# Five gather buffers, a float32 activation in the fronts, and all later column one-hots on ScalarE

## The chip, the core and the metric

The kernel runs on one core of a Trainium2 chip. The metric is the device time of one launch in microseconds (us); the median of three runs is quoted. Beside the timed runs there is one profiled execution, in which the hardware recorded when each instruction ran; all rows in this document come from such executions. The core has five engines that work at the same time, each through its own queue in order: TensorE (PE, matrix products; PEld is its weight load), VectorE (DVE), ScalarE (ACT), GpSimd (POOL), and SyncE (SP), which issues plain transfers. An instruction that waits holds everything behind it in its engine's queue.

## What is computed

One inference step of a two-layer decoder for 512 prompt tokens (four tiles of 128) and 8 sample tokens, all in float32. The first layer mixes tokens by a gated MLP, the second by differential attention. Each is followed by a PEER block: every token picks, for 8 heads, the 16 best of 128 x 128 experts, and adds their outputs. The part that matters here is

```
q = (h @ w_q).reshape(T, 8, 2, 128)
s = einsum('thcd,hcnd->thcn', q, keys)            # two lists of 128 scores per head
sv, si = top_k(s, 16)
cand = sv[:, :, 0, :, None] + sv[:, :, 1, None, :]
top_s, pos = top_k(cand, 16)                       # 16 experts: row key i, column key j
g = softmax(top_s)
act = gelu(einsum('thkd,td->thk', u_tab[eidx], h))
y = einsum('thk,thkd->td', g * act, v_tab[eidx])
```

## The kernel before

Each layer of the kernel (`run_layer`) has fronts and a dense part. A front takes a group of tiles through the token mixing (`gmlp` or `attn`), then through the norm, the query product, the scores and the top-k of the PEER block (`peer_front`). Four fronts are numbered by `stage`: 0 and 1 in the first layer (tile 2; tiles 0, 1, 3 and the samples), 2 and 3 in the second (tile 0; tiles 2, 3, 1 and the samples). A front's products run through `dense`: for each of 8, 16 or 32 columns of weight blocks a 128x1024 block `wt` is loaded and multiplied with the activation, transposed, `hT` (up to 392 tokens wide).

There are two forms of such a product. Where the activation is float32, 8 products go straight from `wt`; the compiler makes two instructions of each. Where it is a pair of float32r halves (`hTh`, `hTl`), `split` makes halves of the weights too (`wh` on ACT, `wl` on DVE), and 24 products of one instruction each are made.

The experts of the tiles are summed in two ways. Two of the four tiles of a layer go through **all** 16,384 experts (`dense_peer`), in four quarters of 32 blocks: `acts(q)` makes gelu(u.h) into `W`, `gates(q)` makes the gate weights by products of one-hots (`gi` for the row keys, `ohj` for the column keys, `ps_g`) and multiplies them into `W`, and the quarter's loop sums `W` times the expert outputs into `y`. While a quarter sums, the next one's `acts` and then `gates` run. The last quarter splits its operands (L562 to L571). The other two tiles are **gathered** (`peer_tile`): 512 times a layer an indirect transfer of 128 rows (0.5 MB) is issued on POOL into a tile `gath`, and one DVE instruction consumes it, L712 for u and L719 for v. The `gath` tiles come from a pool of three buffers, so the third-next transfer waits until DVE has consumed this one.

The order is not written by hand. A scheduler orders each queue, and `pace` ties the n-th gather instruction on DVE to the n-th entry of a list of anchors: `tick(ins, k)` enters an instruction k times. An anchor holds a gather back in the order only; nothing waits for it at run time.

```
gb = ctx.enter_context(tc.tile_pool(name="gb", bufs=3))
...
z = V.scalar_tensor_tensor(u, u, 1.0, h, op0=OP.mult, op1=OP.mult, accum_out=act[:, k:k + 1])
pins[layer].append(z.ins)
...
tick(z, [6, 6, 6, 5][stage[0]])
```

Of the kernel before, what the change touches and what calls it, by code (L numbers as in the profile page):

```python
# [8 lines left out]
F32 = mybir.dt.float32  # L9
# [9 lines left out]
D = 1024  # L19
# [16 lines left out]
def body(ctx: ExitStack, tc: tile.TileContext, a):  # L36
# [4 lines left out]
    gb = ctx.enter_context(tc.tile_pool(name="gb", bufs=3))  # L41
# [35 lines left out]
    HB, NW = [4], [264]  # L77
# [105 lines left out]
    def split_T(name, both=False):  # L183

        if stage[0] == 2 or 1 and not stage[0]:
            return wa.tile([128, 8, 128], F32, name=name, tag="h", bufs=HB[0])
        pool, tag, n = (per, "hT", 392) if stage[0] else (wa, "hA", 256)
        if [0, 0, 0, 0][stage[0]] and not both:
            return pool.tile([128, 8, n], F32, name=name, tag=tag + "h", bufs=1)
        return [pool.tile([128, 8, n], FR, name=name + k, tag=tag + k, bufs=1) for k in "hl"]  # L190
# [20 lines left out]
    def dense(w, nk, rhs, n, consume, f0=0, f1=None, steps=None):  # L211

        f1 = w.shape[0] if f1 is None else f1
        for f in range(f0, f1):
            ps = pm.tile([128, 512], F32, name="ps_d", tag="mm")
            for c0 in range(0, nk, 8):
# [9 lines left out]
                else:  # L226
# [3 lines left out]
                    tick(z, [6, 6, 6, 5][stage[0]])  # L230
# [3 lines left out]
    def to_tok(n, tiles, func, tok):  # L234
        hold = {}

        def consume(ft, ps):
            q, i = divmod(ft, ZF)
            if i == 0:
                hold[0] = wa.tile([128, ZF, NW[0]], F32, name="zT", tag="zT", bufs=3)  # L240
# [23 lines left out]
    def gmlp(tiles, n, ph):  # L264
# [54 lines left out]
        def u_out(ft, ps):  # L319
            if ft % ZF == 0:  # L320
                hold[0] = wa.tile([128, ZF, NW[0]], F32, name="uT", tag="zT", bufs=3)
# [36 lines left out]
    def topk_rank(s, p, nh, state, h0):  # L358
# [14 lines left out]
        cand = wk.tile([128, nh, 88], F32, name="cand", tag=f"cand{nh}", bufs=1)[:p]  # L373
# [92 lines left out]
    def dense_peer(layer, dpa, open_rest, open_odd, smp):  # L466
        hT = dd["hT"]
        NQ, QI, NV = 4, 32, 4
# [4 lines left out]
        def acts(q):  # L473

            W[q] = (odd if q % 2 else dpa).tile([128, QI, 256], F32, name="W", tag="W", bufs=1)
            for il in range(QI):
# [3 lines left out]
                if (il * 5) % 32 < [[0, 16, 32, 32], [0, 16, 32, 32]][layer][q]:  # L480
                    uh, ul = split(u, [2, 3][layer] if q else [0, 1][layer])
                    for c in range(8):
                        PE.matmul(ps, uh[:, c, :], hT[0][:, c, :256], start=c == 0, stop=False)  # L483
                        PE.matmul(ps, uh[:, c, :], hT[1][:, c, :256], start=False, stop=False)  # L484
                    for c in range(8):
                        PE.matmul(ps, ul[:, c, :], hT[0][:, c, :256], start=False, stop=c == 7)  # L486
                else:
                    for c in range(8):
                        for k in range(2):
                            z = PE.matmul(ps[:, k * 128:(k + 1) * 128], u[:, c, :], hF[k][:, c, :], start=c == k == 0,  # L490
                                          stop=c == 7, skip_group_check=True)
                    tick(z, [2, 3][layer] if q else [0, 1][layer])
# [3 lines left out]
        def gates(q):  # L496
# [4 lines left out]
            for t0 in range(0, 256, 32):  # L501
# [32 lines left out]

        hF = [dpa.tile([128, 8, 128], F32, name=f"hF{k}", tag=['vb', 'vb'][k], bufs=3 if ['vb', 'vb'][k] == "vb" else 1)
              for k in range(2)]
        for k in range(2):
            V.tensor_tensor(hF[k], *[z.bitcast(F32)[:, :, k * 128:(k + 1) * 128] for z in hT], op=OP.add)  # L538
# [50 lines left out]
    def peer_front(tiles, n, layer, ph):  # L589
        if any(t == 4 or t not in DT[layer] for t in tiles):  # L590
            gbc = bcast_row(a["f_norm_g"][layer], D, f"g_f{layer}")
        hT = dd["hT"] = split_T("hT", True)
# [23 lines left out]
        if 4 in tiles:  # L616
            qz = [wa.tile([128, 8, 72], F32, name=f"qz{c}", tag="zT", bufs=3) for c in range(2)]
# [82 lines left out]
    def gather(table, ix, k, pool=None, tag="sg", nb=1):  # L700
        t = gb.tile([128, D], F32, name="gath", tag="g") if pool is None else \
            pool.tile([128, D], F32, name="gaths", tag=tag, bufs=nb)
# [64 lines left out]
    def run_layer(layer, setup):  # L767
# [11 lines left out]
        HB[0], NW[0] = 4 - layer, GROUPS[layer][1][1]  # L779
# [58 lines left out]
    def setup1(ph):  # L838
# [182 lines left out]
        def attn(tiles, n):  # L1021
# [6 lines left out]
            if first:  # L1028
                hT = per.tile([128, 8, 392], F32, name="hT", tag="hTh")
# [3 lines left out]
                row4 = per.tile([128, 2, D], F32, name="row4", tag="hTl")[:NB]  # L1033
# [16 lines left out]
            def row(t, k):  # L1050
# [153 lines left out]
```

## Time and profile before

| | us |
|---|---|
| three runs | 3499.5, 3507.37, 3507.73; median 3507.37 |
| the profiled execution, its own time | 3478.04 |
| its span, first to last instruction | 3476.3 |
| busy in the span: PE, DVE, ACT, POOL | 3063.4, 2545.1, 1421.2, 1289.9 |

The profiled execution was 0.8% faster than the median of the runs. Busy times of different engines overlap. A busy PE is not a PE at its pace: the ends of matrix products are modelled, and consecutive ones overlap in the records, as DVE's do by some 0.08 us. In the rows, "x<-ps_b" means that x was written from ps_b, and "<-DVE hF L538" behind a time in brackets or a bar names what ended the wait.

### The profile page before, as it was taken

The page shows a single profiled execution, that of the slowest core. Times are in us where ns is not written, and L with a number is a line of the kernel's source. Part 1 is how long each engine was busy: PE and PEld are TensorE (multiplying, and loading weights), DVE is VectorE, ACT ScalarE, POOL GpSimd, SP SyncE. Part 2 cuts the span into 40 slices and gives each one's busy share as a digit, 9 for nine tenths or more (in the row PEclk, how much of TensorE's full clock was granted, in tenths as well). Part 3 has the DMA queues.
Part 4 walks back from the last instruction along what each step waited for, and adds up shares of the span by engine and source line. Part 5 has one row for each costly group of instructions (what it writes and reads, how often), then busy time and mean ns, then how long its engine had stood idle before and what let it go on. Part 6 is the DMA issues. An engine that isn't in the chain of part 4 may idle for free.

```text
span 3476.3 us, 53629 instructions
## 1 busy us (share of the span) xinstructions
PE 3063.4 (88%) x19776; PEld 2450.6 (70%) x19776; DVE 2545.1 (73%) x5191; ACT 1421.2 (41%) x3180; POOL 1289.9 (37%) x1061
## 2 busy tenths in 40 slices
PE   7988948779999999999888888646899999999998
PEld 7887538779757857757878643546899658758656
DVE  1478569888666777668657677779888666777778
ACT  2343022125565485664444344322236334343433
POOL 0034442334344344434320433442334444334343
PEclk9998979889999999999999988769899999999999
DMA  7677875778888989889985777775788889889888
GB/s 257 226 253 253 276 241 189 254 277 284 299 310 308 332 304 320 318 292 327 332 287 179 281 256 248 261 235 176 270 301 311 313 300 321 318 291 341 304 278 316
DMA packets 271576, 976.76 MB, mean 281 GB/s; under 512 B 30938, under 2 KB 31770, under 8 KB 271306
## 3 DMA queue, kind: packets, MB, share of 16 engines
q0 software_dynamic: 152064, 553.72, 46.5%
q1 hardware_dynamic: 119250, 419.62, 34.5%
q8 instruction: 155, 2.54, 0.3%
q14 instruction: 107, 0.88, 0.1%
HBM read 966.76 MB, written 6.46 MB: 280 GB/s over the span
## 4 chain that ended last, share of the span: by engine, by line
PE 37%; DMA 27%; DVE 15%; issue 14%; POOL 6%; ACT 1%; POOLq 0%; DVEq 0%; SPq 0%; ACTq 0%
DMA gath<-peer_v,ix 15%; PE y L573 10%; DMA gath<-peer_u,ix 9%; POOL gath L703 6%; PE ps_d L228 4%; DVE gath L712 3%; PE ps_g L528 3%; DVE x L719 3%; PE ps_a L486 3%; PE ps_a L490 3%; PE ps_a L483 3%; PE ps_a L484 3%; PE y L570 1%; DVE wl L208 1%; PE y L571 1%
## 5 line engine op out<-in xcount | busy, mean ns | idle before, releaser
L703 POOL DMA_INDIRECT gath<-peer_u,ix x512 | 634.2, 1239 | 1212.4 <-DVE gath L712 631.1
L703 POOL DMA_INDIRECT gath<-peer_v,ix x512 | 612.6, 1197 | 910.4 <-DVE x L719 531.4
L712 DVE SCALAR_TENSOR_TENSOR gath<-gath,h_g 128x1024 f32<-128x1024 f32 x512 | 622.9, 1222 | 298.0 <-DMA gath<-peer_u,ix 295.9
L719 DVE SCALAR_TENSOR_TENSOR x<-gath,act,x 128x1024 f32<-128x1024 f32 x512 | 656.2, 1282 | 246.1 <-DMA gath<-peer_v,ix 241.5
L573 PE MATMUL y<-vb,W 128*128 128x512 f32 x1536 | 718.6, 611 | 5.2 <-DVE W L531 5.2
L521 ACT ACTIVATE ohj<-iota,selJ 128x128 f16<-128x128 f32 x1408 | 423.8, 388 | 352.0 <-PE ps_g L528 351.7
L573 PEld LDWEIGHTS y<-vb,W 128*128 128x128 f32 x1536 | 285.4, 196 | 292.6 <-issue 287.2
L490 PE MATMUL ps_a<-hF,ub 128*128 128x128 f32 x3072 | 362.5, 281 | 50.9 <-DVE hF L538 50.3
L490 PEld LDWEIGHTS ps_a<-hF,ub 128*128 128x128 f32 x3072 | 358.6, 198 | 52.7 <-DVE hF L538 50.7
L528 PEld LDWEIGHTS <-ohj 128*128 128x128 f16 x4096 | 257.6, 130 | 94.1 <-issue 86.5
L483 PE MATMUL ps_a<-hTh,wh 128*128 128x256 f32 x1280 | 320.3, 288 | 0.0
L484 PE MATMUL ps_a<-hTl,wh 128*128 128x256 f32 x1280 | 312.4, 282 | 0.0
L528 PE MATMUL ps_g<-gi,ohj 128*128 128x32 f16 x4096 | 269.9, 233 | 11.6 <-DVE gaths L731 8.1
L206 ACT ACTIVATE wh<-ub 128x1024 fp32r<-128x1024 f32 x160 | 169.6, 1060 | 255.0 <-PE ps_a L484 205.0
L483 PEld LDWEIGHTS ps_a<-hTh,wh 128*128 128x128 f32 x1280 | 243.1, 190 | 3.4 <-issue 2.9
L484 PEld LDWEIGHTS ps_a<-hTl,wh 128*128 128x128 f32 x1280 | 242.7, 190 | 3.4 <-issue 3.4
L222 PE MATMUL ps_d<-hTh,wh 128*128 128x392 f32 (+1 forms) x640 | 230.7, 362 | 12.2 <-ACT qT L637 5.3
L223 PE MATMUL ps_d<-hTl,wh 128*128 128x392 f32 (+1 forms) x640 | 226.4, 355 | 3.5 <-DVE hTl L200 3.2
L208 DVE TENSOR_TENSOR wl<-ub,wh 128x1024 fp32r<-128x1024 f32 x160 | 194.9, 1222 | 43.2 <-ACT wh L206 37.8
L531 DVE TENSOR_TENSOR W<-ps_g,W 128x512 f32<-128x512 f32 x128 | 156.7, 1225 | 83.0 <-PE ps_g L528 82.5
L493 ACT ACTIVATE W<-ps_a 128x256 f32<-128x256 f32 x256 | 94.7, 374 | 275.1 <-PE ps_a L490 217.8
L206 ACT ACTIVATE wh<-wt 128x1024 fp32r<-128x1024 f32 x88 | 93.3, 1061 | 242.5 <-PE ps_d L223 168.3
(313 smaller groups left out, 4662.0 us busy)
## 6 DMA issues: line engine op xcount, KB each, us to landing
ub<-peer_ut SPq DMA_DIRECT2D x256, 512.0 KB, 5.2
vb<-peer_v SPq DMA_DIRECT2D x256, 512.0 KB, 5.3
wt<-w_in SPq DMA_DIRECT2D x64, 512.0 KB, 4.5
wt<-peer_wq SPq DMA_DIRECT2D x64, 512.0 KB, 4.3
wt<-w_out SPq DMA_DIRECT2D x32, 512.0 KB, 4.5
gath<-peer_u,ix POOLq DMA_INDIRECT x512, 6.1
gath<-peer_v,ix POOLq DMA_INDIRECT x512, 6.2
wt<-w_k SPq DMA_DIRECT2D x16, 512.0 KB, 5.6
```

What stands on the lines that cost most here:

```text
L206: SC.activation(wh, w, AF.Copy)
L208: tick(V.tensor_tensor(wl, w, wh.bitcast(F32), op=OP.subtract), k)
L222: PE.matmul(ps[:, :n], wh[:, c, :], rhs[0][:, c, :n], start=c == 0, stop=False)
L483: PE.matmul(ps, uh[:, c, :], hT[0][:, c, :256], start=c == 0, stop=False)
L484: PE.matmul(ps, uh[:, c, :], hT[1][:, c, :256], start=False, stop=False)
L490: z = PE.matmul(ps[:, k * 128:(k + 1) * 128], u[:, c, :], hF[k][:, c, :], start=c == k == 0, stop=c == 7, skip_group_check=True)
L521: SC.activation(oh[:, :, k], iota128, AF.Abs, scale=-1.0, bias=selJ[:, t2 + k:t2 + k + 1])
L528: PE.matmul(ps[:, t - t1, :], oh[:, :, k], gi[:, c, :, t - t0], start=c == 0, stop=c == 1)
L573: PE.matmul(y[t][hf], w[:, ts], v[:, hs], start=i == 0, stop=i == 127)
L703: GP.indirect_dma_start(out=t, out_offset=None, in_=table, in_offset=bass.IndirectOffsetOnAxis(ap=ix[:, k:k + 1], axis=0))
L712: z = V.scalar_tensor_tensor(u, u, 1.0, h, op0=OP.mult, op1=OP.mult, accum_out=act[:, k:k + 1])
L719: z = V.scalar_tensor_tensor(x[t], v, act[:, k:k + 1], x[t], op0=OP.mult, op1=OP.add)
```

## The change

The pool of gather buffers has five instead of three. The activation of the query product, and in the second layer of the products by w_k, w_v and w_o as well, is one float32 tile (`full_T`, in the pool `wk`) instead of a pair of halves; only the input product of stage 1 keeps the halves. Of 88 splits of front weights 32 stay. The first quarter's `acts` use that tile in one product of 256 tokens (`hT`) instead of two of 128 (`hF0`, `hF1`, which DVE had to add up first); the later quarters use halves `hP`, made while the second block of the first quarter runs, and all their blocks are split, where half of the second quarter's were not: 192 splits of `ub` instead of 160. From the second quarter on every column one-hot is made on ACT (L521, L524: eight narrow instructions and one wide), where in the second layer half were one DVE instruction each (L515): 80 become 32. The anchors of stage 1's query product grow from 2 to 6 per column of blocks, those of stage 3 become 3. The rest moves memory: three `h` tiles instead of four in the first layer, two `zT` tiles instead of three there, and `row4` goes into the `h` ring.

```
-    gb = ctx.enter_context(tc.tile_pool(name="gb", bufs=3))
+    gb = ctx.enter_context(tc.tile_pool(name="gb", bufs=5))
...
-    HB, NW = [4], [264]
+    HB, NW, ZB = [3], [264], [3]
...
+    def full_T(name):
+
+        if stage[0] % 2 == 0:
+            return wa.tile([128, 8, 128], F32, name=name, tag="h", bufs=HB[0])
+        return wk.tile([128, 8, 392], F32, name=name, tag="hT", bufs=1)
+
+    def split_T(name):
+
+        if stage[0] != 1:
+            return full_T(name)
+        return [pool.tile([128, 8, 392], FR, name=name + k, tag="hT", bufs=1) for k, pool in (("h", wk), ("l", wa))]
...
-                    tick(z, [6, 6, 6, 5][stage[0]])
+                    tick(z, [6, 6, 6, 3][stage[0]])
...
+        hP = [dpa.tile([128, 8, 256], FR, name=f"hP{k}") for k in "hl"]
...
-                if (il * 5) % 32 < [[0, 16, 32, 32], [0, 16, 32, 32]][layer][q]:
-                    uh, ul = split(u, [2, 3][layer] if q else [0, 1][layer])
+                if q:
+                    uh, ul = split(u, [2, 3][layer])
...
-                        for k in range(2):
-                            z = PE.matmul(ps[:, k * 128:(k + 1) * 128], u[:, c, :], hF[k][:, c, :], start=c == k == 0,
-                                          stop=c == 7, skip_group_check=True)
+                        z = PE.matmul(ps, u[:, c, :], hT[:, c, :256], start=c == 0, stop=c == 7)
...
+                    if il == 1:
+                        SC.activation(hP[0], hT[:, :, :256], AF.Copy)
+                        V.tensor_tensor(hP[1], hT[:, :, :256], hP[0].bitcast(F32), op=OP.subtract)
...
-                        if (t2 // 8) % 4 < ([2, 2][layer] if not q else 2 * J_DVE[layer][q]):
+                        if not q and (t2 // 8) % 4 < 2:
...
-        hT = dd["hT"] = split_T("hT", True)
+        hT = dd["hT"] = full_T("hT")
...
-        HB[0], NW[0] = 4 - layer, GROUPS[layer][1][1]
+        HB[0], NW[0], ZB[0] = 3, GROUPS[layer][1][1], 2 + layer
...
-                hT = split_T("hT")
+                hT = full_T("hT")
...
-            oT = split_T("oT")
+            oT = full_T("oT")
```

What the scheduler makes of it, first on DVE at the norm before stage 3's query product: `rs_...` and `r` are the steps of the norm's root, `gath,act<-gath,h_g` is a gather's u instruction. Before:

```order
L128 TENSOR_SCALAR rs_msm<-ss 128x4
L129 TENSOR_SCALAR rs_ym<-rs_msm 128x4
L712 SCALAR_TENSOR_TENSOR gath,act<-gath,h_g 128x1024
L134 TENSOR_TENSOR rs_tm<-rs_ym 128x4
L135 TENSOR_TENSOR rs_tm<-rs_tm,rs_msm 128x4
L712 SCALAR_TENSOR_TENSOR gath,act<-gath,h_g 128x1024
L137 SCALAR_TENSOR_TENSOR rs_ym<-rs_tm,rs_ym 128x4
L134 TENSOR_TENSOR rs_tm<-rs_ym 128x4
L135 TENSOR_TENSOR rs_tm<-rs_tm,rs_msm 128x4
L712 SCALAR_TENSOR_TENSOR gath,act<-gath,h_g 128x1024
L138 SCALAR_TENSOR_TENSOR rs_um<-rs_tm 128x4
L140 SCALAR_TENSOR_TENSOR r<-rs_um,rs_ym 128x4
```

The same place after the change:

```order
L128 TENSOR_SCALAR rs_msm<-ss 128x4
L129 TENSOR_SCALAR rs_ym<-rs_msm 128x4
L134 TENSOR_TENSOR rs_tm<-rs_ym 128x4
L135 TENSOR_TENSOR rs_tm<-rs_tm,rs_msm 128x4
L137 SCALAR_TENSOR_TENSOR rs_ym<-rs_tm,rs_ym 128x4
L134 TENSOR_TENSOR rs_tm<-rs_ym 128x4
L135 TENSOR_TENSOR rs_tm<-rs_tm,rs_msm 128x4
L138 SCALAR_TENSOR_TENSOR rs_um<-rs_tm 128x4
L140 SCALAR_TENSOR_TENSOR r<-rs_um,rs_ym 128x4
L607 SCALAR_TENSOR_TENSOR h_g<-x_78,r,g_f_18047 128x1024
```

The gathers have left the root's steps; here they stand ahead of the last additions to x and behind the norm. Second, DVE at the end of the program, in the last quarter, before (`wl` and `wdl` are the low halves that PE multiplies, `x_78<-gath,act,x_78` a gather's v instruction):

```order
L564 TENSOR_TENSOR wdl<-W,wdh 128x256
L208 TENSOR_TENSOR wl<-vb,wh 128x1024
L719 SCALAR_TENSOR_TENSOR x_78<-gath,act,x_78 128x1024
L564 TENSOR_TENSOR wdl<-W,wdh 128x256
L208 TENSOR_TENSOR wl<-vb,wh 128x1024
L719 SCALAR_TENSOR_TENSOR x_78<-gath,act,x_78 128x1024
```

And after:

```order
L565 TENSOR_TENSOR wdl<-W,wdh 128x256
L211 TENSOR_TENSOR wl<-vb,wh 128x1024
L565 TENSOR_TENSOR wdl<-W,wdh 128x256
L211 TENSOR_TENSOR wl<-vb,wh 128x1024
L565 TENSOR_TENSOR wdl<-W,wdh 128x256
L211 TENSOR_TENSOR wl<-vb,wh 128x1024
```

No gather is left in either layer's last quarter. Counted over DVE's whole queue, the gather instructions (L712 and L719) are spread so; the times are those at which the profiled execution of before passed the marks:

| DVE's queue from ... to ... | us of before | gathers before | after |
|---|---|---|---|
| first gather to the norm before stage 1's query product | 196 to 482 | 103 | 108 |
| to the first multiply of the gates into W (L531) | 482 to 784 | 81 | 121 |
| to the 16th of 64 such multiplies | 784 to 912 | 42 | 45 |
| to the 64th | 912 to 1567 | 211 | 238 |
| last quarter of the first layer, and stage 2 | 1567 to 1830 | 75 | 0 |
| stage 3, to the 9th head's softmax | 1830 to 2033 | 46 | 60 |
| to its 32nd, the last | 2033 to 2173 | 50 | 75 |
| to the norm before stage 3's query product | 2173 to 2285 | 41 | 29 |
| to the second layer's first multiply into W | 2285 to 2584 | 87 | 80 |
| to its 64th | 2584 to 3368 | 253 | 268 |
| last quarter of the second layer | 3368 to 3476 | 35 | 0 |

Between the last multiply of one quarter's gates and the first of the next, where `acts` stands, 38, 37, 38 and 36 gathers become 46, 45, 46 and 47.

## Rows read from the trace of the kernel before

**Rows 1.** The page's first part: busy us, share of the span, instructions.
```profile
PE 3063.4 (88%) x19776; PEld 2450.6 (70%) x19776; DVE 2545.1 (73%) x5191; ACT 1421.2 (41%) x3180; POOL 1289.9 (37%) x1061
```
**Rows 2.** The waits: engine, line, releaser; us in total, times, longest us.
```profile
POOL gath L703 <- DVE gath L712: 732.2, 331, 19.5
...
DVE gath L712 <- DMA gath<-peer_u,ix: 295.9, 212, 4.6
...
DVE x L719 <- DMA gath<-peer_v,ix: 241.5, 198, 6.0
```
**Rows 3.** The DMA issues: count, median us from issue to landing.
```profile
gath<-peer_u,ix POOLq DMA_INDIRECT x512, 6.1
```
**Rows 4.** Busy us (instructions) per stretch: PE, PEld, DVE, ACT, POOL; PEclk, DMA share, GB/s.
```profile
160.00:482.00 322.00, 260.44 (x1272) 217.95 (x1272) 225.69 (x422) 87.05 (x147) 130.69 (x106) 0.90 0.78 261
482.00:784.00 302.00, 230.18 (x1644) 223.89 (x1645) 263.36 (x945) 74.53 (x142) 102.00 (x82) 0.86 0.69 235
784.00:912.00 128.00, 128.00 (x1331) 126.56 (x1330) 107.24 (x128) 81.76 (x205) 53.76 (x42) 1.00 0.82 284
912.00:1662.00 750.00, 727.19 (x4380) 506.58 (x4380) 532.04 (x667) 444.74 (x1038) 316.18 (x257) 0.98 0.89 315
1662.00:1830.00 168.00, 142.21 (x1091) 132.95 (x1090) 94.45 (x218) 77.37 (x210) 47.31 (x41) 0.92 0.83 298
1830.00:2033.00 203.00, 175.93 (x956) 148.24 (x954) 146.66 (x405) 80.49 (x176) 56.25 (x49) 0.94 0.70 236
2033.00:2173.00 140.00, 117.68 (x353) 50.92 (x354) 107.78 (x289) 55.31 (x146) 54.48 (x51) 0.79 0.79 257
2173.00:2285.00 112.00, 55.70 (x277) 50.33 (x275) 84.01 (x131) 31.32 (x46) 52.34 (x41) 0.68 0.77 254
2285.00:2584.00 299.00, 227.44 (x1624) 217.97 (x1625) 270.23 (x950) 73.93 (x140) 105.49 (x89) 0.88 0.72 243
2584.00:3368.00 784.00, 769.12 (x5357) 568.81 (x5355) 581.69 (x723) 322.77 (x745) 332.68 (x268) 0.98 0.88 310
3368.00:3476.30 108.30, 94.92 (x384) 74.61 (x384) 91.57 (x118) 41.98 (x63) 37.40 (x32) 0.94 0.86 305
```
**Rows 5.** Timeline of DVE, 2272 to 2286 us: start, us, what [idle before <-releaser].
```profile
2272.63 1.23 DVE L712 SCALAR_TENSOR_TENSOR gath<-gath,h_g 128x1024 f32<-128x1024 f32 x1 [3.92 <-DMA gath<-peer_u,ix]
...
2276.99 0.17 DVE L128 TENSOR_SCALAR rs_msm<-ss 128x4 f32<-128x4 f32 x1
...
2284.74 0.16 DVE L140 SCALAR_TENSOR_TENSOR r<-rs_um,rs_ym 128x4 f32<-128x4 f32 x1
```
**Rows 6.** PE's waits: us in total, times, longest us.
```profile
PE ps_t L172 <- ACT xr L168: 58.0, 3, 24.9
PE ps_a L490 <- DVE hF L538: 50.3, 2, 25.6
...
PE ps_t L196 <- DVE hTl L179: 26.4, 3, 13.3
```
**Rows 7.** Timeline of PE at 378 and 2255 us: float32 and halves, 392 tokens.
```profile
378.03 6.42 PE L228 MATMUL ps_d<-uv,wt 128*128 128x392 f32 x19
...
2255.71 1.59 PE L225 MATMUL ps_d<-oTh,wl 128*128 128x392 f32 x8
```
**Rows 8.** Groups by line: count | busy us, mean ns of one | idle before.
```profile
L712 DVE SCALAR_TENSOR_TENSOR gath<-gath,h_g 128x1024 f32<-128x1024 f32 x512 | 622.9, 1222 | 298.0 <-DMA gath<-peer_u,ix 295.9
L521 ACT ACTIVATE ohj<-iota,selJ 128x128 f16<-128x128 f32 x1408 | 423.8, 388 | 352.0 <-PE ps_g L528 351.7
...
L524 ACT ACTIVATE ohj<-ohj 128x1024 f16<-128x1024 f16 x176 | 179.6, 1044 | 0.5
...
L208 DVE TENSOR_TENSOR wl<-wt,wh 128x1024 fp32r<-128x1024 f32 x88 | 107.5, 1221 | 11.6 <-ACT wh L206 5.6 <-ACT kq_tok L1044 3.5 <-ACT uv L276 2.2
...
L515 DVE TENSOR_TENSOR ohj<-selb,iotaJ 128x1024 f16<-128x1024 f16 x80 | 54.8, 687 | 19.6 <-PE ps_g L528 19.4
```
**Rows 9.** Busiest stretch of the transfers, same columns as Rows 4.
```profile
1425.00:1440.00 15.00, 15.00 (x109) 12.04 (x108) 12.09 (x15) 4.94 (x9) 6.65 (x6) 1.00 0.99 376
```

More of the change, by code (lines that the diff above doesn't have):

```diff
@@ L239, in consume @@
             if i == 0:
-                hold[0] = wa.tile([128, ZF, NW[0]], F32, name="zT", tag="zT", bufs=3)
+                hold[0] = wa.tile([128, ZF, NW[0]], F32, name="zT", tag="zT", bufs=ZB[0])
             z = hold[0]
@@ L320, in u_out @@
             if ft % ZF == 0:
-                hold[0] = wa.tile([128, ZF, NW[0]], F32, name="uT", tag="zT", bufs=3)
+                hold[0] = wa.tile([128, ZF, NW[0]], F32, name="uT", tag="zT", bufs=ZB[0])
             u = hold[0]
@@ L372, in topk_rank @@
                 yield
-        cand = wk.tile([128, nh, 88], F32, name="cand", tag=f"cand{nh}", bufs=1)[:p]
+        cand = wk.tile([128, nh, 88], F32, name="cand", tag="cand", bufs=1)[:p]
         def add(o, a0, na, nb):
@@ L532, in gates @@
                     yield
[L535 to L538, printed above, removed]
         for _ in acts(0):
@@ L616, in peer_front @@
         if 4 in tiles:
-            qz = [wa.tile([128, 8, 72], F32, name=f"qz{c}", tag="zT", bufs=3) for c in range(2)]
+            qz = [wa.tile([128, 8, 72], F32, name=f"qz{c}", tag="zT", bufs=ZB[0]) for c in range(2)]
             for z in qz:
@@ L698, in sample_finish, with gather @@
         yield
-    def gather(table, ix, k, pool=None, tag="sg", nb=1):
+    def gather(table, ix, k, pool=None):
         t = gb.tile([128, D], F32, name="gath", tag="g") if pool is None else \
-            pool.tile([128, D], F32, name="gaths", tag=tag, bufs=nb)
+            pool.tile([128, D], F32, name="gaths", tag="sg", bufs=1)
         GP.indirect_dma_start(out=t, out_offset=None, in_=table,
@@ L1028, in attn @@
             if first:
-                hT = per.tile([128, 8, 392], F32, name="hT", tag="hTh")
+                hT = wk.tile([128, 8, 392], F32, name="hT", tag="hT", bufs=1)
                 zb = hT[:, :, nq:nq + 256]
@@ L1032, in attn @@
                 hT = hT[:, :, :nq]
-                row4 = per.tile([128, 2, D], F32, name="row4", tag="hTl")[:NB]
                 smp["v"] = ks.tile([128, D], F32, name="v_smp", tag="hs", bufs=1)[:NB]
@@ L1048, in heads, with row @@
                 return [(dst[t][:rows[t]].rearrange("p (h d) -> p h d", d=64), rows[t]) for t in kqv]
-            def row(t, k):
-                return wa.tile([128, D], F32, name="kq_tok", tag="h", bufs=HB[0]) if t < 4 else row4[:, k]
-            kt = {t: row(t, 0) for t in kqv}
+            def row(t):
+                return wa.tile([128, D], F32, name="kq_tok", tag="h", bufs=HB[0])[:rows[t]]
+            kt = {t: row(t) for t in kqv}
             dense_tok(a["w_k"], 8, hT, nq, kqv, AF.Copy, rows_out(kt))
@@ L1062, in attn @@
                     to_T(kt[t], NB, smp["kT"], 0)
-            qt = {t: row(t, 1) for t in kqv}
+            qt = {t: row(t) for t in kqv}
             dense_tok(a["w_q"], 8, hB, nq, kqv, AF.Copy, rows_out(qt))
```

14 lines of the change are left out of this document (4 added, 10 removed).

## The prediction

> **What bounds the kernel now.** I read the busy times first. PE is busy for 88% of the span, DVE for 73%, ACT for 41% [rows 1]; that names no bound yet, since the stages differ. So I cut the span into stretches [rows 4]. In the two dense stretches, 912 to 1662 and 2584 to 3368 us, PE is busy for 727 of 750 and 769 of 784 us: PE sets them. In the fronts it isn't: from 482 to 784 PE has 230 of 302 us, from 2285 to 2584 227 of 299, while DVE has 263 and 270. In these two DVE sets the time (top-k, splits, gathers), and PE waits for what DVE does last. The other stretches are chains: between 2173 and 2285 neither PE (56 of 112) nor DVE (84) is full.
>
> Next the waits. POOL waits 732 us for DVE to give back a gather buffer, at the u gathers alone, and DVE waits 296 + 242 = 538 us for gathered rows [rows 2]. A gather lands 6.1 us after its issue [rows 3] and its DVE instruction takes 1.22 us [rows 8]; with three buffers a round of at least 7.3 us brings three gathers, 2.4 us each, beside a mean of 3.2 (1,024 over the 3,270 us from the first on). The order was made for that pace, and DVE, in order, stands still at each late one with all that is behind it. Where it hurts is seen at the norm ahead of stage 3's query product [rows 5]: nine small steps of 0.16 us, yet between 2272.63 and 2284.90 DVE gets through them only among six gathers, the first after an idle 3.92 us. PE waits for that norm's result: 58 us at three such places, 50 us twice for the sum `hF`, 26 us for the low halves `hTl` [rows 6].
>
> **The change, stretch by stretch.** I sum against the profiled execution, 3478 us; the runs' median is 0.8% above it, and I carry the same difference over to it.
>
> Prices first. A column of blocks with float32 costs PE 6.42 us for 19 instructions, the last one's own 0.5 us included, so 0.329 each and 16 of them 5.26 us; by halves the last eight take 1.59 us, 0.179 each, and 24 of them 4.29 us [rows 7]. So each of the 56 changed columns costs PE 0.97 us **more**, 54 us in all: 16 in stage 1, 40 in stage 3. In return DVE loses 1.22 us per split [rows 8], ACT about as much. A one-hot costs ACT 8 x 0.30 (424 us busy over 1,408) + 1.04 = 3.4 us instead of DVE 0.69 [rows 8]: 48 of them put 165 us on ACT and take 33 off DVE. ACT has 323 of 784 us there; the first layer's later quarters already make all of theirs on ACT, with ACT at 445 of 750 and PE at 97% [rows 4]. I cost this edit at zero, hidden beside PE; if ACT were too late, its bound is the 165 us less what fits, and the first layer speaks for nothing.
>
> *160 to 482.* Five gathers more, but no late ones: two norms have their root among gathers here, and each loses some 8 us of the 12 that rows 5 show. **-16** (bounds -5 and -25; PE's idle time here is 62).
>
> *482 to 784.* DVE sets it. Removed: 16 splits, 19.5 us, and 20 low halves, an estimated 8 us (each writes an eighth to a half of what a split writes in 1.22 us). Added: 40 gathers (81 become 121, since the anchors of stage 1 grow from 2 to 6), at 1.22 us: 49. DVE goes from 263 to 285. Its idle 39 us are mostly late gathers; I leave 23. 308: **+6** (-15, +25). PE's first `acts` start some 25 us earlier without `hF`, for nothing: the gates need DVE's top-k. The 15.5 us more of products are hidden in the same wait.
>
> *784 to 912.* DVE 107 of 128. 13 splits more (all blocks of the second quarter), 16 us, and three gathers, 4: 127. Idle 21 becomes 9: **+8** (-5, +15). PE's savings there give nothing, because DVE is then last.
>
> *912 to 1662.* PE sets it. 38 gathers leave the last quarter, where DVE, with splits and gathers, is what PE waits for; the second layer's shows the price: PE 95 of 108 us, so 12 to 13 us for 35. **-13**. Against it, 16 gathers more stand in the two `acts` pieces, where transfers are densest: 8.4 MB (0.524 each), or 22 us at the 376 GB/s of the busiest stretch [rows 9]; I charge 4 of the 22, since the stretch as a whole has 11% of the transfers' time free [rows 4]. **-9** (-20, +20).
>
> *1662 to 1830.* All 37 gathers go, 45 of DVE's 94 us, and some 20 MB of transfers with them. PE is idle for 26 us; part of that is its own chain. **-11** (0, -20).
>
> *1830 to 2285.* To 2033: 16 columns of stage 3, +15.5 on PE, against half of PE's idle 27: +2. To 2173: 25 gathers more, +31 on DVE's 108, so it nearly fills the 140, and with 13 idle makes 152: +12. To 2285: eight columns, +8; DVE falls from 84 to 54 (8 splits, 8 low halves, 12 gathers less), the norm's root is free of gathers, the transposes need no low half; I take half of PE's idle 56 back: -20. **-6** (-30, +25).
>
> *2285 to 2584.* Like 482 to 784, but the anchors give seven gathers less instead of 40 more. DVE: 16 splits, 20 low halves, 7 gathers, 36 us less: 234, and with half its idle time 249. PE: 227 + 15.5, and 14 for the norm and the transposes: 257. PE is later. **-42** (-20, -55). The 25 us of `hF` and most of the waits for `r` and `hTl` go here.
>
> *2584 to 3368.* 13 splits more and four gathers fewer up to the 16th multiply, 11 us on a DVE that has idle time there: +2; 19 gathers more in the two `acts` pieces, 10 MB or 26 us, of which 6: **+8** (-5, +30). *Last quarter*: **-12** (-5, -15).
>
> Sum: -16 + 6 + 8 - 9 - 11 - 6 - 42 + 8 - 12 = **-74**. 3478 becomes 3404, the median 3507 becomes **3433**. The bounds are independent, so their spread adds in squares: about 50 either way.
>
> **The rivals.**
>
> *DVE gets freer than I think.* Five buffers take away nearly all 538 us of waits. Then 482 to 784 ends 15 us earlier instead of 6 later, 784 to 912 5 earlier, 160 to 482 saves 25, 1830 to 2285 15 more, the last quarters 6 more: 21 + 13 + 9 + 15 + 6 = 64 beyond the forecast, 3369. For it: a round of 7.3 us over five buffers is 1.5 us a gather. Against it: the new order spends the pace at once, 121 gathers in 302 us.
>
> *A deeper queue only lengthens.* If gathers land later in proportion to their number in flight (10 us instead of 6.1), five buffers are as late as three. Then the 16 at 160 to 482 are lost, the idle time that I took off at 482 to 912 (16 and 12) and at 2285 to 2584 (14), and 10 at 2173: 68 of the 74, so 3472, 3501 for the median, and the change does not do what it says. Against it: in the fronts the transfers' engines are busy for 69 to 78% at 235 to 261 GB/s [rows 4], far from 376.
>
> *The transfers are the bound in `acts`.* If those pieces have no room left, the 35 gathers more (18.4 MB) cost their full 49 us at 376 GB/s instead of my 10: -35, 3472 for the median. For it: 0.99 of the engines' time in the busiest stretch [rows 9]. The Trainium skill, DMA: Bandwidth & Descriptors, section Bandwidth, speaks for it too: for transfers from HBM the HBM side binds, at about 358 GB/s for a core; the row's 376 GB/s lies a little above, so the ceiling it names is about where the trace has one, and 18.4 MB would be an estimated 51 us by it.
>
> *PE holds the fronts* (the other side). If PE and not DVE is what ends the fronts, the float32 columns outside 482 to 784 cost their 40 x 0.97 = 39 us openly, and the 75 us that I book in the fronts (16, 11, 6, 42) do not come: 3478 + 1 + 39 = 3518, the median 3547. It decides from the point where PE's idle time in 1830 to 2584, now 177 us, falls by less than 39. For it: float32 is dearer on PE by 23%. Against it: those 177 us [rows 4].
>
> **How the numbers follow.** Forecast (own range 3385 to 3480) 0.50; freer DVE 0.17; transfers in `acts` 0.12; longer queue 0.10; PE 0.11. A difference under 0.3%, some 10 us, can't be told from none here. Faster by more: 0.50 + 0.17 + 0.12 and a third of the longer queue, 0.82; same 0.08; slower 0.10. For 8 in 10 the range goes from 3370, the freer DVE, to 3510, past the longer queue.
>
> **What would show it.** DVE's waits for `gath` fall from 538 to under 200 us, with a landing time under 8 us. The wait for `hF` is gone, and 2285 to 2584's counterpart takes about 257 us, with PE's idle time there halved; 482 to 784's is unchanged within 15. Stage 2 and the last quarters hold no gather, and PE is at 95% or more in the latter. ACT is under 75% in the second layer's gates. Wrong would be: landings of 9 us or more, PE idle in `acts` with waits for `ub` or `wl`, or query products that run without a gap and end later than before.

## The result, and the profile after

The changed kernel takes 3346.91 us (median; 3341.34 to 3354.19, four runs) against 3507.55 us (3499.5 to 3510.39, four runs): ratio 0.9547, 95% interval 0.9523 to 0.9571. It is 161 us faster, where 74 were forecast, and lies 23 us under the range. Its profiled execution took 3354.19 us, 124 less than the one that the forecast was summed on. The direction was right and the size was not.

The page's first part:

```profile
PE 3083.2 (92%) x18048; PEld 2315.2 (69%) x18048; DVE 2464.0 (73%) x5045; ACT 1537.9 (46%) x3586; POOL 1374.2 (41%) x1061
```

Against [rows 1] PE rose from 88% to 92% of a shorter span. The waits of the changed kernel (us in total, times, longest us):

```profile
POOL gath L704 <- DVE x L720: 510.1, 219, 17.9
POOL gath L704 <- DVE ix L672: 490.2, 2, 304.4
POOL gath L704 <- DVE gath L713: 382.8, 185, 14.3
...
DVE gath L713 <- DMA gath<-peer_u,ix: 99.1, 84, 7.5
DVE x L720 <- DMA gath<-peer_v,ix: 49.7, 47, 3.3
...
ACT W L499 <- DVE si L369: 41.7, 2, 23.2
...
PE ps_a L494 <- ACT W L499: 29.3, 2, 16.6
```

DVE's waits for gathered rows are 99 + 50 = 149 us where they were 538 [rows 2]. The stretches, from mark to mark as in [rows 4]:

```profile
161.00:438.00 277.00, 254.49 (x1286) 215.38 (x1284) 228.77 (x434) 85.53 (x145) 157.01 (x111) 0.96 0.86 309
438.00:751.80 313.80, 243.78 (x1050) 185.78 (x1051) 288.88 (x972) 62.65 (x134) 159.84 (x125) 0.86 0.84 300
751.80:881.00 129.20, 119.81 (x1147) 115.21 (x1145) 124.15 (x152) 90.27 (x207) 73.79 (x46) 0.96 0.86 301
881.00:1638.00 757.00, 740.80 (x4456) 522.24 (x4455) 534.52 (x665) 452.77 (x1085) 312.45 (x248) 0.97 0.84 307
1638.00:1768.00 130.00, 122.06 (x1024) 115.81 (x1024) 38.61 (x143) 61.49 (x169) 0.00 (x0) 0.99 0.63 205
1768.00:1963.00 195.00, 183.07 (x823) 123.93 (x821) 139.96 (x380) 61.75 (x155) 82.62 (x65) 0.96 0.82 290
1963.00:2128.00 165.00, 132.94 (x375) 58.68 (x374) 138.00 (x337) 60.89 (x157) 93.99 (x74) 0.73 0.86 299
2128.00:2201.00 73.00, 54.13 (x198) 34.13 (x198) 53.51 (x87) 17.43 (x30) 37.58 (x30) 0.85 0.82 295
2201.00:2478.70 277.70, 240.77 (x1006) 180.31 (x1007) 240.40 (x914) 60.93 (x129) 98.02 (x81) 0.91 0.73 258
2478.70:3255.00 776.30, 764.36 (x5207) 557.71 (x5205) 584.98 (x706) 492.87 (x1190) 357.62 (x278) 0.97 0.87 318
3255.00:3352.50 97.50, 92.02 (x384) 73.52 (x384) 52.78 (x67) 41.96 (x62) 0.00 (x0) 0.97 0.46 151
```

The largest single surprise is the first: 322 us became 277. PE was busy for 260 of the 322 us [rows 4] and is for 254 of the 277; its products in there are the same but for the ends of the window. DVE, by line, in that stretch, in the kernel before and then in the changed one:

```profile
L712 DVE SCALAR_TENSOR_TENSOR gath<-gath,h_g 128x1024 f32<-128x1024 f32 x55 | 67.2, 1225 | 52.0 <-DMA gath<-peer_u,ix 51.7
L719 DVE SCALAR_TENSOR_TENSOR x<-gath,act,x 128x1024 f32<-128x1024 f32 x48 | 61.6, 1283 | 39.1 <-DMA gath<-peer_v,ix 38.4
L208 DVE TENSOR_TENSOR wl<-wt,wh 128x1024 fp32r<-128x1024 f32 x34 | 41.5, 1221 | 3.8 <-ACT uv L276 2.2 <-ACT wh L206 1.4 <-issue 0.2
```

```profile
L713 DVE SCALAR_TENSOR_TENSOR gath<-gath,h_g 128x1024 f32<-128x1024 f32 x60 | 72.3, 1220 | 21.1 <-DMA gath<-peer_u,ix 20.7
L720 DVE SCALAR_TENSOR_TENSOR x<-gath,act,x 128x1024 f32<-128x1024 f32 x48 | 61.5, 1281 | 12.1 <-DMA gath<-peer_v,ix 11.2
L211 DVE TENSOR_TENSOR wl<-wt,wh 128x1024 fp32r<-128x1024 f32 x32 | 39.1, 1221 | 8.0 <-ACT uv L279 4.1 <-ACT wh L209 2.7 <-issue 0.7
```

The work is nearly the same (five gathers more and two splits fewer fall into the window). What differs is the last column: 90 us of waits for rows became 32, and of those 58 us 45 are off the stretch.

Below are the same marks on DVE's timeline (those of the table in the section on the change, named by the times of before) for five kernels; the runs are told in the next section. Lengths in us.

| stretch of before | forecast | before | before, again | changed | changed, again | three buffers | late order, five | no gather transfers |
|---|---|---|---|---|---|---|---|---|
| 0 to 482 | -16 | 482 | 491 | 438 | 437 | 493 | 438 | 441 |
| 482 to 784 | +6 | 302 | 305 | 314 | 314 | 312 | 277 | 294 |
| 784 to 912 | +8 | 128 | 128 | 129 | 129 | 124 | 123 | 118 |
| 912 to 1567 | -20, with the next | 655 | 661 | 653 | 654 | 641 | 633 | 633 |
| 1567 to 1830 | | 263 | 262 | 234 | 233 | 256 | 250 | 233 |
| 1830 to 2285 | -6 | 455 | 465 | 433 | 435 | 495 | 445 | 404 |
| 2285 to 2584 | -42 | 299 | 309 | 278 | 277 | 301 | 275 | 270 |
| 2584 to 3368 | +8 | 784 | 785 | 776 | 776 | 770 | 748 | 751 |
| last quarter | -12 | 109 | 107 | 98 | 98 | 104 | 97 | 97 |
| span | -74 | 3476 | 3512 | 3352 | 3350 | 3497 | 3285 | 3241 |

### The profile page after: what moved, and what is told of

It is laid out like the page before. It is cut to its first block, busy times and chain, and to the rows that moved or that the text cites. A ratio compares the mean times of both kernels' runs of the same rounds, so it can differ in the third digit from the quotient of the medians.

```text
span 3352.5 us, 50442 instructions
## 1 busy us (share of the span) xinstructions
PE 3083.2 (92%) x18048; PEld 2315.2 (69%) x18048; DVE 2464.0 (73%) x5045; ACT 1537.9 (46%) x3586; POOL 1374.2 (41%) x1061
## 4 chain that ended last, share of the span: by engine, by line
PE 64%; DVE 12%; DMA 9%; issue 7%; POOL 4%; ACT 4%; SPq 0%; DVEq 0%; POOLq 0%; ACTq 0%
PE y L574 19%; PE ps_d L231 7%; PE ps_g L534 6%; PE ps_a L488 5%; PE ps_a L489 5%; PE ps_a L491 5%; DMA gath<-peer_u,ix 4%; POOL gath L704 4%; PE ps_a L494 3%; DMA gath<-peer_v,ix 3%; DVE gath L713 2%; DVE x L720 2%; PE y L570 2%; PE y L571 2%; PE y L572 2%
## 5 line engine op out<-in xcount | busy, mean ns | idle before, releaser
L527 ACT ACTIVATE ohj<-iota,selJ 128x128 f16<-128x128 f32 x1792 | 543.8, 388 | 150.4 <-PE ps_g L534 140.9
L231 PE MATMUL ps_d<-hT,wt 128*128 128x128 f32 (+3 forms) x2048 | 430.3, 369 | 25.1 <-DMA wt<-peer_wq 6.8
L488 PE MATMUL ps_a<-hPh,wh 128*128 128x256 f32 x1536 | 402.0, 298 | 11.1 <-ACT wh L209 11.1
L231 PEld LDWEIGHTS ps_d<-hT,wt 128*128 128x128 f32 x2048 | 304.4, 199 | 136.7 <-issue 16.9
L489 PE MATMUL ps_a<-hPl,wh 128*128 128x256 f32 x1536 | 384.7, 287 | 0.0
L488 PEld LDWEIGHTS ps_a<-hPh,wh 128*128 128x128 f32 x1536 | 300.5, 196 | 23.2 <-ACT wh L209 12.7
L489 PEld LDWEIGHTS ps_a<-hPl,wh 128*128 128x128 f32 x1536 | 300.5, 196 | 8.4 <-issue 8.4
L494 PE MATMUL ps_a<-hT,ub 128*128 128x256 f32 x1024 | 234.9, 392 | 29.7 <-ACT W L499 29.3
L494 PEld LDWEIGHTS ps_a<-hT,ub 128*128 128x128 f32 x1024 | 200.4, 197 | 60.8 <-ACT W L499 30.1
L530 ACT ACTIVATE ohj<-ohj 128x1024 f16<-128x1024 f16 x224 | 231.0, 1043 | 0.2
```

The lines of the kernel that those rows point to most:

```text
L231: z = PE.matmul(ps[:, :n], wt[:, c, :], rhs[:, c0 + c, :n], start=c0 + c == 0, stop=c0 + c == nk - 1)
L488: PE.matmul(ps, uh[:, c, :], hP[0][:, c, :], start=c == 0, stop=False)
L489: PE.matmul(ps, uh[:, c, :], hP[1][:, c, :], start=False, stop=False)
L494: z = PE.matmul(ps, u[:, c, :], hT[:, c, :256], start=c == 0, stop=c == 7)
L527: SC.activation(oh[:, :, k], iota128, AF.Abs, scale=-1.0, bias=selJ[:, t2 + k:t2 + k + 1])
L530: SC.activation(oh2, oh2, AF.Relu, bias=1.0, scale=-1.0)
```

## The experiments

**Which part makes the gain.** Two theories stood against each other, A: the buffers; B: the float32 activation, the moved gathers and the one-hots. First the changed kernel with three buffers:

```
-    gb = ctx.enter_context(tc.tile_pool(name="gb", bufs=5))
+    gb = ctx.enter_context(tc.tile_pool(name="gb", bufs=3))
```

> The changed kernel with three gather buffers instead of five and nothing else edited. Theory A (the buffers made most of the gain, because the vector engine's queue stood at late gathers and all of the fronts' work stood behind them): its waits for gathered rows return from 149 us to 400 or more, the stretch from the first gathers to the norm ahead of stage 1's query product, where the change left the products as they were, returns from 277 towards 320 us, and the median lies between 3420 and 3480 us. Theory B (the float32 activation, the moved gathers and the one-hots made it, and five buffers only help): the stretch stays under 290 us and the median lies between 3350 and 3390 us.

3501.27 us (ten runs), ratio to before 0.9997 (0.9976 to 1.0018): without the buffers the whole change is worth nothing. It is above A's own range. DVE's waits:

```profile
DVE gath L713 <- DMA gath<-peer_u,ix: 305.1, 217, 7.1
...
DVE x L720 <- DMA gath<-peer_v,ix: 278.7, 197, 5.1
```

584 us, more than before had. B falls, and the same edit with `bufs=4` shows how fast the gain comes:

> The changed kernel with four gather buffers. At 7.3 us for a round, four buffers allow a gather each 1.8 us, five each 1.5 us, three each 2.4 us, beside a mean of 3.2 us between gathers and 2.6 us in stage 1's query product. Theory A: most of the gain is there with four, as 1.8 lies under both: 3350 to 3385 us, waits for gathered rows 180 to 280 us. If bursts in the order count more than the mean pace, the median lies half way between three and five buffers, 3390 us or more. Theory B: within 10 us of five buffers.

3375.34 us, ratio 0.964 (0.9613 to 0.9667), waits 165 + 106 = 271 us, both within A's ranges. The fourth buffer brings 126 us, the fifth 28.

Then the float32 activation, first with three buffers, and in stage 1 alone with five:

```
-        if stage[0] != 1:
+        if stage[0] % 2 == 0:
             return full_T(name)
...
-        hT = dd["hT"] = full_T("hT")
+        hT = dd["hT"] = split_T("hT")
```

> Three gather buffers, and the query products of stages 1 and 3 and the products by w_k, w_v and w_o made from a pair of halves again (with the same number of gathers tied to each column; the first quarter's acts keep one float32 product, from the sum of the halves). Against the run with three buffers it prices the float32 activation alone. Theory A: the vector engine is held by gathers in both, so 56 splits more change little: 0 to 20 us longer than with three buffers, near the kernel before. Theory B: 40 us or more longer than with three buffers. By the matrix engine's own price, 54 us less work, it could be shorter, by 10 us at most, if that engine set the fronts.

3503.4 us against 3501.27 on the same chip: no difference.

> The changed kernel, five buffers, with stage 1's query product from a pair of halves again (16 columns; six gathers tied to each as in the changed kernel; the first quarter's acts of that layer use the sum of the halves). With three buffers the float32 activation was worth nothing. Theory A1 (it is worth something only once the gathers are on time, because then the vector engine is busy 289 of the 314 us of this stretch): 16 splits at 1.22 us and the low halves, an estimated 27 us, are added to a full engine, and the median is 15 to 30 us longer than that of the changed kernel, 3360 to 3375. Theory A2 (the buffers alone count): within 10 us of 3347.

3361.45 us (3350.47 to 3366.02), ratio 0.9584 (0.9531 to 0.9636), which overlaps the changed kernel's interval; the stretch of the query product takes 321 us instead of 314, though 111 gathers stand in it instead of 121. It leans to A1 and doesn't settle it. The second layer's columns with five buffers weren't tried.

The one-hots, half of them on DVE again:

```
-                        if not q and (t2 // 8) % 4 < 2:
+                        if (t2 // 8) % 4 < (2 if not q else 2 * J_DVE[layer][q]):
```

> The changed kernel with half of the second layer's later column one-hots on the vector engine again, as before (80 there instead of 32). The prediction booked this edit at nothing. If that holds: within 10 us of the changed kernel. If the vector engine's 33 us less in the second layer's gates are part of the 8 us that this stretch came out shorter: 5 to 20 us longer than the changed kernel, all between the first and the last multiply of the gates. If the scalar engine's 165 us more cost something there: shorter than the changed kernel by 5 us or more.

3341.46 us, ratio 0.9539 (0.9507 to 0.9571): nothing, as booked. Between the first and the last multiply of the gates it is 24 us shorter, and from there to the end 21 longer, but that is the mark alone: DVE ends its last multiply at 3224.7 us, 23 us before PE comes to the last quarter (0.5 us in the changed kernel). The quarter's products then take PE 90 us with most of the 15 gathers behind it, against 92.

**Was the profile of before a typical one?** The kernel before, unedited:

> The kernel before, profiled once more, unedited. The execution that the forecast was summed on, 3478 us, lay under every timed run of this kernel. If it was a lucky one: this profile comes out at 3495 to 3512 us, and the 20 to 30 us more stand in the fronts, where the vector engine waits for gathers, not in the dense stretches that the matrix engine sets. If its stretches agree with the first profile within 5 us, the difference lies outside the span or in the way of measuring.

3513.97 us, 2 above the range that was named for a lucky first profile; its span is 3512.3. Its waits:

```profile
DVE gath L712 <- DMA gath<-peer_u,ix: 298.7, 210, 4.6
...
DVE x L719 <- DMA gath<-peer_v,ix: 268.3, 199, 5.5
```

567 us, 29 more than in the first profile, and the span is 36 longer: in the two columns of the table the fronts have 32 of the 36 (9, 3, 10 and 10). The first profile was a lucky one: 3478 us lies under every timed run of this kernel. The places are those expected, but for 912 to 1567, which is 6 us longer.

**Where the gathers stand.** The 121 gathers in stage 1's query product looked like the price of the change, so fewer were tied to its columns:

```
-                    tick(z, [6, 6, 6, 3][stage[0]])
+                    tick(z, [6, 6 if nk > 8 else 2, 6, 3][stage[0]])
```

> The changed kernel with two gathers instead of six tied to each column of stage 1's query product, as before; the gathers fall back to later places, some into stage 2 and the last quarter. This stretch now has 121 gathers and takes 314 us with the vector engine busy for 289; its counterpart in stage 3 has 80 and takes 278. If the vector engine sets it: some 40 gathers or 49 us less there, 25 to 35 us shorter, of which the last quarter takes 11 back: 3320 to 3335 us. If the added gathers cost nothing where they stand: 3347 or more, by the 11 of the last quarter.

> As the run before, with four instead of six. By the same reckoning half of it: the stretch 12 to 18 us shorter and less handed to the last quarter, 3330 to 3340 us. If the last quarter stays free of gathers and stage 2 takes them, it could be as good as two.

3340.28 and 3347.58 us. With two, the stretch takes 276 us with 76 gathers, 37 less, but 46 gathers are then in the first layer's last quarter, where the time to stage 2's norm grows from 104 to 119; net 7 us, less than forecast. With four the stretch takes 302 us and the kernel gains nothing, which misses its range too. On one chip, five runs each, and with the one-hots' edit added:

> The changed kernel unedited, to be compared on one chip with the next run: 3340 to 3355 us.

> The changed kernel with two gathers instead of six tied to each column of stage 1's query product, and half of the second layer's later column one-hots on the vector engine, the two edits that came out 7 and 5 us below it, each on another chip. If both are real and add: 3330 to 3338 us, 8 to 15 us below the changed kernel on the same chip. If they are spread between chips: within 5 us of it.

3348.11 and 3335.63 us, 12 us apart, as for two edits that add: real, and small.

The floor, with no gather transfers at all (`gather` returns one tile of zeros):

> The changed kernel with the 1,024 gather transfers left out: the vector engine's gather instructions work on one tile of zeros, so the gathered tiles' expert sums are missing from the output, and nothing waits for a row. It gives the floor under any number of buffers. The 149 us of waits that are left are partly beside other waits: if half of them are on the path, 3260 to 3300 us. If the 537 MB less of transfers also shorten the matrix engine's waits for blocks, lower, to 3220. If five buffers have already taken all that there is: 3320 or more.

3238.6 us, under 3260: more than half of the waits were on the path. By its time it is the case with shorter waits for blocks, but not by its reason, for PE's waits for transfers sum to 18 us in both profiles. 108 us of the changed kernel still hang on the gathers' transfers.

**Order or waits.** Five buffers change two things: at run time a transfer may start earlier, and the scheduler, which knows the buffers, places the gathers earlier on DVE. This edit gives it an entry that says that a transfer follows the gather instruction two before it; no semaphore comes of it, so five buffers act at run time in about the order of three. By the trace, the 257th gather stands behind 1361 other DVE instructions (the reads of accumulators not counted); with three buffers it is behind 1362, in the changed kernel behind 1311.

```
+        used = pins[0] + pins[1]
+        for d, z in zip(gds[2:], used):
+            tc.add_manual_dep(d, z.name, NOSYNC, reason="three")
```

> The changed kernel, five buffers, with an entry for the scheduler alone that lets each gather's transfer follow the gather instruction two before it; nothing waits for that at run time. On the vector engine the gathers then stand about as late in the order as with three buffers (the 129th behind 459 other instructions, 436 with three buffers, 401 in the changed kernel; the 449th behind 1261, 1257 and 1199). It tells the order from the waits. If the gain comes from rows that are there in time: waits for gathered rows under 200 us, and 3345 to 3385 us, the upper end for the gathers that fall back into the last quarters. If it comes from the order that five buffers make possible: 3480 to 3510 us, as with three.

**3279.92 us** (3270.33 to 3286.99), ratio 0.9348 (0.9317 to 0.938), 67 us under the changed kernel. Both expectations fell: the order doesn't make the gain, and it isn't neutral either; the early order gives part of the gain back. The runs that follow ask how. The lateness of the entry was varied (`gds[3:]`, `gds[1:]`), and the buffers with the late order were cut to four:

> Five buffers, with each gather's transfer put after the gather instruction three before it, for the scheduler alone. The order is then about that of four buffers (the 129th gather behind 431 other instructions; 459 in the late order, 401 in the changed kernel). If the gain falls with the order's lateness: between 3280 and 3347, 3305 to 3330 us.

> Five buffers, with each gather's transfer put after the gather instruction just before it, for the scheduler alone. The gathers then stand so late that 145 of the first layer's come in a bunch ahead of the second layer and 129 of the second's at its end. If lateness alone were good: under 3280. If the gathers must also find work to stand beside: 150 gathers at the end, at 1.3 us each, have nothing beside them but the last quarter, and the time is 3330 us or more.

> Four buffers with the scheduler's entry of the run with the late order (each gather's transfer after the gather instruction two before it). Against that run, 3280 us, it changes only how far ahead a transfer can start. If slack counts, the number of buffers beyond those that the order was made for: one spare instead of two, waits for rows 200 to 300 us, 3310 to 3350 us. If any order that is later than the buffers force gives the whole gain: 3290 us or less.

3289.38 us (ratio 0.9398, 0.9369 to 0.9427), 3755.37 us and 3328.73 us (0.9521, 0.9496 to 0.9547). The first is below its range: the order of about four (the 257th gather behind 1333 instructions, 1336 with four buffers) gives nearly the whole gain. The last is within the range for slack, with 226 us of waits. The latest order loses at the two places that were named, stage 2 with the gathers ahead of it and the last quarter (columns as in [rows 4]):

```profile
1543.00:2010.00 467.00, 170.51 (x1327) 160.34 (x1326) 316.88 (x667) 88.03 (x244) 239.15 (x189) 0.69 0.84 291
3374.00:3744.70 370.70, 91.39 (x384) 73.07 (x384) 286.56 (x353) 43.17 (x68) 229.38 (x183) 0.62 0.87 300
```

194 and 188 gathers stand there, with PE busy for 171 of 467 and 91 of 371 us. The other runs fall into one table: median us, and in brackets DVE's waits for rows.

| order made for about | three buffers at run time | four | five |
|---|---|---|---|
| three | 3501 (584) | 3329 (226) | 3280 (126) |
| four | | 3375 (271) | 3289 (130) |
| five | | | 3347 (149) |

Along a row the order is about the same and a buffer brings 172, then 49 us. Down a column, with the buffers fixed, an order made for one buffer less is 47 or 58 us faster, for two less 67.

Last, whether the late order gains only by taking gathers out of stage 1's query product:

> The late order with five buffers and two gathers instead of six tied to each column of stage 1's query product. There the late order already holds 98 gathers instead of 121 and takes 277 us instead of 314, as long as the run with fewer anchors took with 76. If that stretch's gain is the same one: within 6 us of 3280. If it adds: 3265 us or less.

3278.64 us: the two don't add in sum. Its profile shows the query stretch shorter (263 us); the stretch that ends with stage 2 is 36 us longer and the one behind it 39 shorter.

## Why the prediction was wrong

*The direction and the mechanism* stood: the waits for rows fell from 538 to 149 us, as "under 200" asked, and with three buffers all of the gain is gone. Of the rivals, "DVE gets freer than I think" (3369) was the nearest. "A deeper queue only lengthens" falls: in pairs of the n-th issue and the n-th gather instruction, where DVE sat idle for over 0.3 us before it, the median from issue to use was 7.0 us with three buffers (375 pairs, before again) and 7.9 with five (125 pairs, changed again). That is a microsecond longer, not in proportion. The landing time isn't in the later pages, but it can be worked out from the packets in the traces: each gather closes with 16 packets of 4 bytes, and taken in order, the last of them ends a median of 5.8 us after the issue in both profiles of before (where the page has 6.1) and 6.4 in both of the changed kernel, under the 8 that was asked. "PE holds the fronts" falls with the ratio, and PE's idle time in 1830 to 2584 fell from 177 us to 100. "The transfers are the bound in `acts`": the dense stretches came out 2 to 10 us shorter, not longer. The Trainium skill, DMA: Bandwidth & Descriptors, section Bandwidth, names about 358 GB/s as what binds transfers from HBM for a core, as its share when both cores of a pair stream. The changed kernel moved 331 between its 16th and 64th multiply, which lies under it and tells nothing against it; the 376 of [rows 9] lie above it.

*The step that failed is the term "160 to 482: -16".* I gave five buffers 8 us at each of two roots, after the picture of [rows 5], with -25 as the bound. The stretch gave 44 us, 55 against the repeated profile. The two places were right and too small, and the rest of the stretch was left out. PE's waits in it, with the one that ends at each norm, in the kernel before and then in the changed one:

```profile
PE ps_t L172 <- ACT xr L168: 24.8, 1, 24.8
PE ps_mix L305 <- ACT uv L285: 22.7, 2, 21.9
PE ps_b L248 <- DVE x L259: 8.5, 2, 5.1
PE ps_d L222 <- DVE uv L308: 4.7, 3, 2.1
PE ps_b L248 <- DVE xs_t L259: 1.2, 1, 1.2
```

```profile
PE ps_t L172 <- ACT xr L168: 12.4, 1, 12.4
PE ps_mix L308 <- ACT uv L288: 10.4, 2, 9.6
```

ACT scales `uv` by the root that ended at 270, and `xr` by the one before stage 1's query product. PE's waits for them fell by 12.3 and 12.4 us, 25 in all, where I had 16. With three buffers in the changed kernel they are 22.6 and 29.0. The roots' own steps, at which I had looked, hardly show it (5.4 us became 2.9, and 1.7 became 2.8): the late gathers stood mostly ahead of them. Another 14 us are PE's waits for DVE's additions to `x` and `xs_t` and for its `uv`, which stand among the gathers too; none of them is left, and I had charged nothing there. The last 6 us are PE's busy time, at a mean granted clock of 0.96 instead of 0.90. DVE's queue set this stretch: its work and its waits for rows were 226 + 90 of the 322 us. There a wait for a row was worth most of its length: between the marks at 270 and 482 the idle time ahead of DVE's gather instructions, summed over its timeline, fell by 41 us (67 to 26) and the time by 34. Between 912 and 1567, where PE was full, it fell by 109 (134 to 25) and the time by 2. I had the rule (DVE, in order, stands still with all that is behind it) and then charged only the places that I had looked at.

*1830 to 2285: -6* was mis-sized in the same way: -22, or -30 against the repeated profile, where the idle time ahead of its gathers fell by 27, or 39. The parts were right in sign: 2033 to 2173 gave +25 for the forecast +12, and 2173 to 2285 gave -39 for -20.

*2285 to 2584: -42* was too much: -21 or -32. I had PE later, at 257. Neither PE (241 of 278) nor DVE (240) is full, and the run without transfers still takes 270, so a chain bounds it that the transfers don't touch. A part of it is seen in the waits: `hF` is gone, but PE's first `acts` wait for ACT's first write of `W` instead (29 us at two places, where `hF` had 50), and that write waits for the last `si` of DVE's top-k. Freed of one late input, `acts` met the next.

*The dense stretches: charged +4 and +6 for denser transfers.* Against the kernel before no such cost came, though both take 20 and 25 us less without gather transfers. *784 to 912, +8*: +1. *482 to 784, +6*: +11, as forecast in kind; with 45 gathers fewer, 55 us of DVE's time, the run with two anchors a column took 37 us less there. *The last quarters and stage 2*: -9 to -29, near the forecast; but the reason was off. In the late order 22 gathers stand in the second layer's last quarter, and it takes 97.3 us, as long as with none. Thus the 13 us that I booked for "DVE is what PE waits for" were waits, not instructions. Where gathers stood in stage 2 and ahead of it the cost was real: 67 of them, 250 us instead of 234.

*The scaling.* I carried the profile's 0.8% over to both sides. Profile against profile the change gave 124 us; between the repeated profiles (3512.3 and 3350.4) it gave 162, and 161 between medians. So 37 of the 87 us that I missed lie in the two profiles: that of before was 30 us under the median of its runs, that of the changed kernel 7 above. The first had 29 us less of waits for rows than its repeat; in the changed kernel's two profiles these waits are 149 and 152.

*Float32 and one-hots*, the largest part of my working, are worth little here: the one-hots nothing, as booked, float32 nothing with three buffers; with five, stage 1's columns may be worth some 15 us, which isn't settled. By its shape, the float32 tile takes half the memory of a pair. That this is what makes room for two more buffers isn't shown; with stage 1's pair they did fit.

*What is not settled* is why the early order costs 67 us, with waits that differ by 23 (149 and 126). By the table, 37 us lie in stage 1's query product, 20 and 28 in the dense stretches and 9 elsewhere, and between 1567 and 2285 the late order gives 28 back. In the dense stretch from the 16th to the 64th multiply, of the changed kernel, of the late order, and of the kernel without transfers:

```profile
881.00:1534.00 653.00, 641.18 (x4019) 441.11 (x4017) 477.93 (x586) 402.00 (x986) 312.45 (x248) 0.97 0.90 331
```

```profile
838.00:1470.50 632.50, 631.21 (x4015) 435.60 (x4013) 437.42 (x529) 402.08 (x981) 261.16 (x218) 0.99 0.89 315
```

```profile
852.00:1485.00 633.00, 631.79 (x4028) 438.01 (x4028) 475.95 (x577) 404.62 (x989) 22.51 (x15) 0.99 0.46 147
```

The second has 203 gathers, the first 238, the third 233 instructions without transfers. So it isn't DVE's 35 instructions that cost the 20 us: the third has 30 of them and is as short as the second. It is the transfers, or the waits for them (25 us of idle time ahead of DVE's gather instructions in the first, 11 in the second, 4 in the third). On PE the 20 us are two halves: it is idle for 12 us instead of 1, and about the same products keep it busy 10 us longer. Its granted clock is at the lower of its two levels, 1.2 instead of 2.4 GHz, for 38 us in the first and 14 in each of the others, which is the mean of 0.97 or 0.99. PE's waits in the first:

```profile
PE ps_g L534 <- ACT ohj L530: 7.4, 4, 2.2
PE y L574 <- DVE W L537: 1.6, 1, 1.6
PE ps_hb L729 <- DVE W L537: 1.5, 1, 1.5
```

None is a wait for a block of weights or its halves; they are for ACT's one-hots and DVE's multiplies, and the second has none of them. So the idle half is lost by way of these two queues; which instruction makes them late, and what brought the lower clock, isn't shown. In the second layer's dense stretch (776 and 748 us) PE is likewise idle for 12 us instead of 3 and busy 19 us longer, with 46 us instead of 3 at the lower clock. In stage 1's query product, where DVE is nearly full, the sum closes: 23 gathers less at 1.22 us and 9 us less of waits are 37, the whole difference between 314 and 277.

## What to carry to other kernels

Price a late input by the queue, not by the place where it is seen. Where the work and the waits of an in-order engine fill a stretch, most of the waiting counted (41 us of waits, 34 of time); where another engine was full, hardly any (109 and 2). So sum the waits stretch by stretch, and read what the other engines wait for, before sizing anything else. A late result is measured from the moment when its inputs were ready, not from its own first step. A buffer that the scheduler knows of is spent in its order; here an order made for one or two buffers less than there were was 47 to 67 us faster, since the spare ones absorb the landing times, and one made later still lost more than the whole gain. And take a second profile of the kernel before, when the first lies outside its timed runs.

## What the runs showed of the hardware

The round from issue to use that I had worked out as 7.3 us was about right with three buffers (medians of 6.4 to 7.0 in three profiles) and grew by about one microsecond with five (7.8 and 7.9), with the transfers' engines busy for 73 to 86% in the fronts instead of 69 to 79. The Trainium skill, DMA: Bandwidth & Descriptors, section Anatomy of one DMA — SWDGE (gpsimd) path, gives 2.0 us and the bytes at 436 GB/s, an estimated 3.2 us for 512 KB by that page; the row's 6.1 us of landing [rows 3] is about twice that, beside other transfers, and the measurement decides. The mean granted TensorE clock rose as PE's idle time in the span fell: 0.926 with 439 us in the repeated profile of before, 0.939 with 269 in the changed kernel, 0.955 with 236 in the late order and 0.961 with 221 without gather transfers.
